# Layer 1's first gate and up tile: from the normalised stream to the residual scaled by channel, with root and shift put in behind

## The chip, the cores and the metric

The kernel runs on one core of one Trainium2 chip. The metric is the device time of one execution in microseconds (us). A core has a matrix engine (TensorE, PE in the profile; its weight loads are PEld), a vector engine (VectorE, DVE), an engine for scalar functions (ScalarE, ACT), a general one (GpSimd, POOL), a queue that issues the transfers (SyncE, SP), and 16 DMA engines. Each engine takes its instructions in the order in which the program put them, and waits where an operand is not there.

## The reference, cut to what matters

A two-layer diffusion transformer on 256 latent and 256 context tokens of 2048 channels. Layer 0 mixes by pooling, layer 1 by neighbourhood attention in which the latent tokens also read the context. Each layer then has a gated feed-forward part with a convolution of three tokens on the gate:

```python
def modulate(x, shift, scale):
    return x * (1 + scale) + shift

def conv_ffn(u, w_gate, w_up, conv_w, conv_b, w_down):
    T = u.shape[1]
    gp = jnp.pad(u @ w_gate, ((0, 0), (1, 1), (0, 0)))
    gte = gp[:, :T] * conv_w[0] + gp[:, 1:T + 1] * conv_w[1] + gp[:, 2:] * conv_w[2] + conv_b
    return (jax.nn.silu(gte) * (u @ w_up)) @ w_down

h = h + ml[:, 2] * y_lat                       # y_lat: the attention's output projection
h = h + ml[:, 5] * conv_ffn(modulate(rms_norm(h, norm2_g[i]), ml[:, 3], ml[:, 4]),
                            ffn_w_gate[i], ffn_w_up[i], ffn_conv_w[i], ffn_conv_b[i], ffn_w_down[i])
```

`rms_norm` divides each token by the root of its mean square and multiplies each channel by a gain. With s the gain times (1 + scale), r the reciprocal root of a token and b the shift, the feed-forward part reads r * (h * s) + b. So its product with a weight W is r * ((h * s) @ W) + b @ W. After layer 1 only the latent tokens are wanted. The gate and up weights have 5504 columns, the down weight 5504 rows.

## The kernel before, in words

Channels lie on the 128 partitions: a stream is 16 tiles of 128 channels by 256 tokens. The residual of the latent tokens, `hl`, stays in SBUF for the whole kernel. Every large product is split in two parts of lower precision: a weight is cast to a high part on ScalarE and the rest is taken off on VectorE, in some places on GpSimd (`split`, L147 and L149). The moving operand is kept as a pair too, high and low part side by side, 512 columns wide. A product with a weight tile of 128 columns is then 16 matmuls of the weight's high part with all 512 columns (here called wide) and 16 of its low part with the 256 high columns (narrow), in two halves of eight channel tiles each: eight wide, eight narrow, eight wide, eight narrow.

Weights come in halves of 512 KB over SP's queue into six staging buffers used in turn (`stage`, `load`). Split halves lie in three pairs of buffers (`whp`), and in three more (`whx`) once the attention's memory is free. PSUM has eight banks: four for gate, up and projections ("gu"), three and one for the rest.

A planner sorts the instructions of each engine at build time. It goes by the order in which the program wrote them and by its own times for when operands are there. `issue_after(x)` sets an instruction behind x on x's engine; `high_priority` lets one go ahead. The list `hold` puts the splits that follow behind given instructions.

Layer 1 runs like this. The attention goes through 16 pairs of heads (`kq_tile`: keys and queries, 3 x 16 and 16 + 16 matmuls); after every fourth pair the values of the next four follow (`v_group`). Keys and queries are rotated with one multiplication on GpSimd each (L937). The scores of a pair are worked off between the next pair's products. Then the output projection: 16 tiles `wo`, each with its update of `hl` (`o_end`, L1112). The last of them, tile 15, multiplies k by k and ends the attention.

The feed-forward norm follows the updates. `Norm.add` squares a tile on ScalarE (L297) and sums it on VectorE (L303). `Norm.rstd` sums over partitions on TensorE (L310), reduces (L313), scales (L314), raises to the power -1/2 on GpSimd (L315), puts the result on a diagonal (L318) and spreads it over all partitions on TensorE (L320). `norm_b` makes the 16 operands `B`: scale by channel and root on VectorE (L754), shift on ScalarE (L755), then the low part, for even tiles on VectorE (L761), for odd ones with one more ScalarE instruction on GpSimd (L758, L759).

`gu1(f)` does the gate and the up product of column tile f (L788 wide, L791 narrow), `gate1(f)` the convolution and the gating, and after every four tiles `down1` multiplies back. In tile 0 both weights are fetched and split ahead of `norm_b`; the splits of their second halves are held behind the last update of `hl` (`hold[:] = [tail]`, L774), those of tile 1 behind the normalised tile 9 (L764).

Of the kernel before, what the change touches and what calls it, by code (L numbers as in the profile page):

```python
# [13 lines left out]
ALU = mybir.AluOpType  # L14
# [45 lines left out]
def kernel(ctx: ExitStack, tc: tile.TileContext, xT, cxT, wmod, wg, wu, wd, wp,  # L60
# [18 lines left out]
    def flat(a):  # L79
        return a.rearrange("p s t -> p (s t)")  # L80
# [205 lines left out]
    class Norm:  # L286


        def __init__(self, streams, pool, name):
            self.streams, self.pool, self.name = streams, pool, name  # L290
            self.n = T * len(streams)
            self.acc = None

        def add(self, h_of, k):
# [439 lines left out]
    tail = _attention(tc, ap0, bank, ld, A, M, hl, wq, wv, wo, rope, strips, ident, v_first)  # L734

    with ExitStack() as ph2:
# [8 lines left out]
        for k in range(KT):  # L745
            n4.add(h_lat, k)
        rstd = n4.rstd()
        B = {}

        def norm_b(ks):  # L750
            for k in ks:
                a = ap0.tile([P, 2, 2, T], F32R, tag=f"A{k}", name=f"B{k}")[:, 0]
                y = f1.tile([P, 512], F32, tag="t2", name=f"nrmB{k}")[:, 0:T]
                nc.vector.scalar_tensor_tensor(y, hl[:, k, :], M(1, 4, k, 0), rstd[:, 0:T], op0=ALU.mult, op1=ALU.mult)  # L754
                nc.scalar.activation(a[:, 0], y, AF.Identity, bias=M(1, 3, k, 0))  # L755
# [8 lines left out]
                if k == 9:  # L764
                    hold[:] = [ins.ins]

        def gu1(f):
            res = []
            pre = None
            if f == 0:  # L770
                pre = [load(lambda a, b: w[1, f][:, a:b], 2048, f"w{nm}1_{f}") for nm, w in (("g", wg), ("u", wu))]
                for q, ts in enumerate(pre):
                    first = split(ts[:1], f"w{q}1_{f}_0", 4)
                    hold[:] = [tail]  # L774
                    pre[q] = first + split(ts[1:], f"w{q}1_{f}_1", 4)
                    hold.clear()
                norm_b(range(KT))
            elif f == 2:
                hold.clear()
            for q, (nm, wsrc) in enumerate((("g", wg), ("u", wu))):  # L780
                parts = pre[q] if pre else ld(wsrc[1, f], f"w{nm}1_{f}", 2 if f % 4 > 1 else 0)
                ps = bank("gu", f"{nm}1_{f}")

                for j in range(2):
                    hi, lo = parts[j]
                    for k in range(8 * j, 8 * j + 8):
                        c = P * (k % 8)
                        nc.tensor.matmul(ps, hi[:, c : c + P], flat(B[k]), start=(k == 0), stop=False)  # L788
                    for k in range(8 * j, 8 * j + 8):
                        c = P * (k % 8)  # L790
                        nc.tensor.matmul(ps[:, T:], lo[:, c : c + P], B[k][:, 0], start=False, stop=(k == KT - 1))  # L791
                res.append(ps)
            return res

        def gate1(f, banks):
            res = []
            for nm, ps in zip("gu", banks):
                e = f1.tile([P, 512], F32, tag="t2", name=f"e{nm}_{f}")[:, 0:T]
                nc.scalar.copy(e, ps[:, T:])
                nc.vector.tensor_tensor(e, e, ps[:, :T], op=ALU.add)  # L800
                res.append(e)
# [101 lines left out]
def _attention(tc, ap0, bank, ld, A, M, hl, wq, wv, wo, rope, strips, ident, v_first):  # L903
# [9 lines left out]
    with ExitStack() as es:  # L913
# [166 lines left out]
        for g in range(4):  # L1080
            v = v_group(g)
            for j in range(4):
# [5 lines left out]
                prev = v, P * j  # L1088
        queue.append(attend(KT - 1, *prev))
# [3 lines left out]
        def x_tile(k):  # L1093
            a = ap0.tile([P, 2, 2, T], F32R, tag=f"A{k}", name=f"oA{k}")[:, 0]
# [159 lines left out]
```

## Time and profile before

| what | value |
|---|---|
| median of three runs | 3057.1 us (3054.04 to 3058.71) |
| profiled execution, its own time | 3053.4 us |
| its span, first to last instruction | 3051.6 us |
| mean granted clock of TensorE | 0.991 |
| TensorE busy | 2974.9 us, 97% |
| VectorE, ScalarE, GpSimd busy | 1932.7, 1372.5, 827.9 us |
| attention's values, keys, queries | about 1690 to 2228 us of the span |
| output projection | about 2228 to 2305 us |
| first gate product of layer 1 | from 2313.12 us |

How to read it: a row of the timeline is the start in us, the duration, the engine, the line, the operation, what it writes and reads with their shapes, and how many instructions were merged. In brackets stands how long the engine had been idle before and which instruction released it. Buffer numbers are left out of names. In the rows of waits: who waited for whom, us in total, times, the longest. The granted clock is the share of full speed that TensorE was given. A busy TensorE counts pipelined matmuls, so times from start to start tell more than durations.

### The profile page before, as it was taken

To read this page: it belongs to the slowest core of one execution; us is meant where nothing else is said; L and a number is where in the kernel's file an instruction comes from. 1 tells how busy PE (TensorE), PEld (TensorE's weight loads), DVE (VectorE), ACT (ScalarE), POOL (GpSimd) and SP (SyncE) were. 2 spreads that over 40 slices of the span, in tenths; PEclk is the share of its full clock that TensorE was granted. 3 is DMA by queue.
4 is the path that set the end of the run, shared out by engine and by line. 5 is a ranking of instruction groups with operands and counts; after the bars stand their busy time and mean duration, and the time that the engine had idled before them with its cause. 6 is when DMAs were issued, how large, how long until landed. Compare 5 with 4: busy or idle time off the path is not lost.

```text
span 3051.6 us, 40877 instructions
## 1 busy us (share of the span) xinstructions
PE 2974.9 (97%) x15082; PEld 2414.5 (79%) x15082; DVE 1932.7 (63%) x2748; ACT 1372.5 (45%) x2219; POOL 827.9 (27%) x823
## 2 busy tenths in 40 slices
PE   5999999999999999999999999999999999999998
PEld 2666668888888888888887887878888888888887
DVE  4455664386584856748576656474767666666666
ACT  4333454324333232333434444343546666666665
POOL 2111313303123030221312000000002566566665
PEclk9999999999999999999999999999999999999999
DMA  9888663374665847557482333333355556655563
GB/s 391 322 308 318 213 213 103 110 249 147 205 202 164 249 137 228 173 186 223 147 251 76 117 100 116 100 106 112 107 162 186 186 185 192 190 186 185 183 194 115
DMA packets 177927, 559.70 MB, mean 183 GB/s; under 512 B 17600, under 2 KB 22208, under 8 KB 177728
## 3 DMA queue, kind: packets, MB, share of 16 engines
q1 hardware_dynamic: 177728, 557.10, 55.9%
q8 instruction: 119, 1.95, 0.2%
q14 instruction: 80, 0.66, 0.1%
HBM read 554.93 MB, written 2.10 MB: 183 GB/s over the span
## 4 chain that ended last, share of the span: by engine, by line
PE 91%; DVE 3%; DMA 3%; POOL 1%; issue 1%; ACT 1%; SPq 0%; DVEq 0%; POOLq 0%; ACTq 0%
PE g L788 5%; PE u L788 5%; PE d L679 5%; PE d L680 5%; PE d L681 5%; PE d L835 4%; PE g L653 4%; PE g L655 4%; PE g L654 4%; PE u L655 4%; PE u L653 4%; PE u L654 4%; PE g L791 3%; PE u L791 3%; PE d L839 2%; PE mod L206 2%
## 5 line engine op out<-in xcount | busy, mean ns | idle before, releaser
L692 POOL TENSOR_TENSOR hl<-hl,dy 128x256 f32<-128x256 f32 x160 | 146.7, 917 | 940.3 <-ACT dy L691 940.1
L850 POOL TENSOR_TENSOR hl<-hl,dy 128x256 f32<-128x256 f32 x320 | 331.6, 1071 | 188.4 <-ACT dy L848 186.1
L262 DVE SCALAR_TENSOR_TENSOR macc<-wm,sc,macc 128x512 f32<-128x512 f32 (+1 forms) x360 | 329.1, 946 | 68.6 <-DMA wm<-wmod 67.6
L691 ACT ACTIVATE dy<-d,modT 128x256 f32<-128x256 f32 x320 | 133.4, 470 | 187.5 <-PE d L681 168.0
L692 POOL TENSOR_TENSOR hc<-hc,dy 128x256 f32<-128x256 f32 x160 | 129.9, 812 | 0.0
L848 ACT ACTIVATE dy<-d,modT 128x512 f32<-128x512 f32 x160 | 104.6, 685 | 42.9 <-PE d L839 41.3
L149 DVE TENSOR_TENSOR wd_2l<-wd,wd_2h 128x1024 fp32r<-128x1024 f32 (+1 forms) x44 | 54.5, 1245 | 107.9 <-ACT wd_2h L147 106.7
L937 POOL TENSOR_TENSOR rk<-rk,rp 128x256 f32<-128x256 f32 x16 | 13.2, 827 | 365.9 <-DVE rk L936 310.2
L206 PE MATMUL mod<-wm,sc 128*32 128x512 f32 x768 | 97.7, 630 | 8.6 <-DMA wm<-wmod 8.4
L149 DVE TENSOR_TENSOR wd_3l<-wd,wd_3h 128x1024 fp32r<-128x1024 f32 (+1 forms) x44 | 52.0, 1202 | 77.7 <-ACT wd_3h L147 76.3
L149 DVE TENSOR_TENSOR wd_1l<-wd,wd_1h 128x1024 fp32r<-128x1024 f32 (+1 forms) x44 | 53.7, 1224 | 60.4 <-ACT wd_1h L147 60.4
L487 POOL TENSOR_TENSOR pf<-ws,inv 128x256 f32<-128x256 f32 x32 | 29.3, 937 | 211.1 <-DVE ws L482 200.8
L147 ACT CAST wd_1h<-wd 128x1024 fp32r<-128x1024 f32 (+1 forms) x44 | 45.3, 1032 | 81.2 <-PE u L654 55.1
L149 DVE TENSOR_TENSOR wd_0l<-wd,wd_0h 128x1024 fp32r<-128x1024 f32 (+1 forms) x44 | 54.6, 1247 | 36.4 <-ACT wd_0h L147 36.2
L1026 ACT ACTIVATE sb<-sb,nm 128x512 f32<-128x512 f32 x64 | 46.1, 721 | 64.3 <-DVE nm L1022 63.2
L147 ACT CAST wd_0h<-wd 128x1024 fp32r<-128x1024 f32 (+1 forms) x44 | 45.2, 1031 | 54.3 <-PE u L788 29.0
L814 DVE TENSOR_TENSOR actb<-sgb,actb 128x256 fp32r<-128x256 f32 x43 | 52.4, 1219 | 27.0 <-ACT actb L813 27.0
L679 PE MATMUL d<-act,wd_2h 128*128 128x512 f32 x172 | 67.1, 390 | 0.0
L680 PE MATMUL d<-act,wd_2h 128*128 128x512 f32 x172 | 66.9, 389 | 0.0
L681 PE MATMUL d<-act,wd_2l 128*128 128x512 f32 x172 | 66.9, 389 | 0.0
L679 PE MATMUL d<-act,wd_0h 128*128 128x512 f32 x172 | 66.9, 389 | 0.0
L680 PE MATMUL d<-act,wd_0h 128*128 128x512 f32 x172 | 66.9, 389 | 0.0
(1752 smaller groups left out, 9220.0 us busy)
## 6 DMA issues: line engine op xcount, KB each, us to landing
wm<-wmod SPq DMA_DIRECT2D x384, 512.0 KB, 6.1
wd<-wd SPq DMA_DIRECT2D x168, 512.0 KB, 4.5
wg<-wg SPq DMA_DIRECT2D x156, 512.0 KB, 4.6
wu<-wu SPq DMA_DIRECT2D x156, 512.0 KB, 4.6
wv<-wv SPq DMA_DIRECT2D x32, 512.0 KB, 3.8
wk<-wq SPq DMA_DIRECT2D x32, 512.0 KB, 3.9
wq<-wq SPq DMA_DIRECT2D x32, 512.0 KB, 3.7
wo<-wo SPq DMA_DIRECT2D x32, 512.0 KB, 4.0
```

The source lines that it names most:

```text
L149: eng.tensor_tensor(lo[:, :n], t[:, :n], hi[:, :n].bitcast(F32), op=ALU.subtract)
L262: nc.vector.scalar_tensor_tensor(acc[s], v, sc2[:, k, s : s + 1], acc[s], op0=ALU.mult, op1=ALU.add)
L653: nc.tensor.matmul(ps, hi[:, c : c + P], xh, start=(k == 0), stop=False)
L654: nc.tensor.matmul(ps, hi[:, c : c + P], xl, start=False, stop=False)
L655: nc.tensor.matmul(ps, lo[:, c : c + P], xh, start=False, stop=(k == KT - 1))
L679: nc.tensor.matmul(ps, hi[:, o : o + P], xh, start=(i == 0), stop=False)
L680: nc.tensor.matmul(ps, hi[:, o : o + P], xl, start=False, stop=False)
L681: nc.tensor.matmul(ps, lo[:, o : o + P], xh, start=False, stop=(i == n - 1))
L692: nc.gpsimd.tensor_tensor(h_of(s)[:, k, :], h_of(s)[:, k, :], y[:, s], op=ALU.add)
L788: nc.tensor.matmul(ps, hi[:, c : c + P], flat(B[k]), start=(k == 0), stop=False)
L791: nc.tensor.matmul(ps[:, T:], lo[:, c : c + P], B[k][:, 0], start=False, stop=(k == KT - 1))
L850: nc.gpsimd.tensor_tensor(hl[:, k, :], hl[:, k, :], y[:, q], op=ALU.add)
```

## The change

While the attention's output projection runs, each updated tile of `hl` is also multiplied by its channel scale and split into a high and a low part. These parts lie in the second half of the buffer whose first half holds the projection's own operand (`xs`). The first gate and up products read them. In the order on TensorE the sums of squares are put behind the first eight wide matmuls and the spread of the root behind the tenth. `norm_b` comes after that and writes its operands for the tiles from 1 on into the first halves. The last two squares are not summed on VectorE but go to TensorE as terms of their own, and the spread takes the root itself, broadcast, times the identity, so that the diagonal's step is gone.

Tile 0's gate and up results are then multiplied by the root and get the product of shift and weight as a bias. This product is made in the attention, once for the gate behind pair 6, once for the up weight behind pair 10 (`shift_row`): the weight tile is loaded once more, multiplied by the shift on GpSimd, added up there to 128 columns, summed over partitions on TensorE, and copied.

Besides: tile 0's splits are no longer held and all on VectorE, tile 1's gate weight is fetched ahead, tile 1 takes the first halves of gate and up before the second halves, and its up weight's split is placed behind tiles of `norm_b`.

```diff
+        def add_stream(self, h_of, k, s):
+            sq = self.pool.tile([P, 512], F32, tag="t2", name=f"{self.name}q{k}_{s}")[:, 0:T]
+            nc.scalar.activation(sq, h_of(s)[:, k, :], AF.Square)
+            if k >= KT - 2:
+                self.ends.setdefault(s, []).append(sq)
+            elif self.acc is None:
+                self.acc = sq
+            else:
+                v = self.acc[:, T * s : T * s + T]
+                nc.vector.tensor_tensor(v, v, sq, op=ALU.add)
+
+        def sums_of(self, s):
+            ps = bank("d", f"{self.name}s{s}")
+            terms = [self.acc[:, T * s : T * s + T]] + self.ends[s]
+            for j in range(2):
+                for i, sq in enumerate(terms):
+                    self.done = nc.tensor.matmul(ps[:, j : j + 1], sq[:, P * j : P * j + P], ones[:, 0:1],
+                                                 start=(i == 0), stop=(i == len(terms) - 1)).ins
+            v = main.tile([P, 4], F32, tag="normv", bufs=2, name=f"{self.name}v{s}")[:, :2]
+            nc.vector.tensor_scalar(v, ps[:, 0:2], 1.0 / D, EPS, op0=ALU.mult, op1=ALU.add)
+            nc.gpsimd.tensor_tensor(v, v, minus_half[:, :2], op=ALU.pow)
+            return v
+
+        def spread(self, s, v):
+            pb = bank("d", f"{self.name}b{s}")
+            for j in range(2):
+                self.done = nc.tensor.matmul(pb[:, P * j : P * j + P], v[:, j : j + 1].broadcast_to([P, P]), ident,
+                                             start=True, stop=True).ins
+            return pb
...
+    def shift_row(q):
+        ts = [t for t, _ in load(lambda a, b: (wg, wu)[q][1, 0][:, a:b], 2048, f"ws{q}")]
+        for j in range(4):
+            v = ts[j // 2][:, 512 * (j % 2) : 512 * (j % 2) + 512].rearrange("p (k c) -> p k c", k=4)
+            nc.gpsimd.tensor_tensor(v, v, modT[1, 12 + j][:, :, 0:1].broadcast_to([P, 4, P]), op=ALU.mult)
+        for j in range(2):
+            v = ts[0][:, 512 * j : 512 * j + 512]
+            nc.gpsimd.tensor_tensor(v, v, ts[1][:, 512 * j : 512 * j + 512], op=ALU.add)
+        for n in (512, 256, 128):
+            nc.gpsimd.tensor_tensor(ts[0][:, 0:n], ts[0][:, 0:n], ts[0][:, n : 2 * n], op=ALU.add)
...
+        ps = bank("d", f"wsum{q}")
+        nc.tensor.matmul(ps[:, 0:1], ts[0][:, 0:P], ones[:, 0:1], start=True, stop=True)
+        nc.vector.tensor_copy(sums[0][:, q : q + 1], ps[:, 0:1])
...
+        def first1():
+            raw = [load(lambda a, b: w[1, 0][:, a:b], 2048, f"w{nm}1_0") for nm, w in (("g", wg), ("u", wu))]
+            pre = [split(ts, f"w{q}1_0") for q, ts in enumerate(raw)]
+            ahead.append(ld(wg[1, 1], "wg1_1"))
...
+            for q in range(2):
+                ps = bank("gu", f"{'gu'[q]}1_0")
                 for j in range(2):
-                    hi, lo = parts[j]
+                    hi, lo = pre[q][j]
                     for k in range(8 * j, 8 * j + 8):
                         c = P * (k % 8)
-                        nc.tensor.matmul(ps, hi[:, c : c + P], flat(B[k]), start=(k == 0), stop=False)
+                        ins = product(ps, hi[:, c : c + P], flat(xs[k][:, 1]), start=(k == 0), stop=False)
+                        if (q, k) == (0, 7):
+                            with tc.issue_after(ins):
+                                v = n4.sums_of(0)
+                            last = n4.done
+                        if (q, k) == (0, 9):
+                            with tc.issue_after(ins):
+                                rstd.append(n4.spread(0, v))
+                            last = n4.done
+                            norm_b(range(KT))
                     for k in range(8 * j, 8 * j + 8):
                         c = P * (k % 8)
-                        nc.tensor.matmul(ps[:, T:], lo[:, c : c + P], B[k][:, 0], start=False, stop=(k == KT - 1))
+                        ins = product(ps[:, T:], lo[:, c : c + P], xs[k][:, 1, 0], start=False, stop=(k == KT - 1))
...
+            for q, j in ((0, 0), (1, 0), (0, 1), (1, 1)) if f == 1 else ((0, 0), (0, 1), (1, 0), (1, 1)):
+                part(q, j)
...
+                if f == 0:
+                    q = len(res)
+                    nc.vector.tensor_tensor(e, e, rstd[0][:, 0:T], op=ALU.mult)
+                    nc.scalar.activation(e, e, AF.Identity, bias=sums[0][:, q : q + 1])
...
+                if j == 2 and 1 <= g < 3:
+                    aside(g - 1)
...
+            a = xs[m][:, 1]
+            nc.scalar.activation(a[:, 0], hl[:, m, :], AF.Copy, scale=M(1, 4, m, 0))
+            nc.vector.scalar_tensor_tensor(a[:, 1], hl[:, m, :], M(1, 4, m, 0), a[:, 0].bitcast(F32),
+                                           op0=ALU.mult, op1=ALU.subtract)
```

`product` is a matmul put behind `last`, so all later matmuls of these two products stand behind the sums, and then behind the spread. `aside` is `shift_row`.

More of the change, by code (lines that the diff above doesn't have):

```diff
@@ L292, in __init__ @@
             self.acc = None
+            self.ends = {}
         def add(self, h_of, k):
@@ L763, in norm_b @@
                 B[k] = a
-                if k == 9:
-                    hold[:] = [ins.ins]
-        def gu1(f):
-            res = []
[L769 to L782, printed above, removed]
+                done_b.append((act.ins, ins.ins))
@@ L900, in _values, with _attention @@
                 nc.tensor.matmul(pv[i], xl, hi[:, c : c + 512], start=False, stop=(k == KT - 1))
[L903 removed]
+def _attention(tc, ap0, bank, ld, A, M, hl, wq, wv, wo, rope, strips, ident, v_first, xs, aside):
     nc = tc.nc
```

53 lines of the change are left out of this document (46 added, 7 removed).

## The prediction

> **What bounds the kernel now.** I read the page's busy table first, then TensorE's waits from the attention to the first tiles of layer 1's feed-forward part, then that seam in order of time.
>
> ```profile
> span 3051.6 us, 40877 instructions
> PE 2974.9 (97%) x15082; PEld 2414.5 (79%) x15082; DVE 1932.7 (63%) x2748; ACT 1372.5 (45%) x2219; POOL 827.9 (27%) x823
> ...
> PE g L788 <- DVE B L761: 2.2, 1, 2.2
> PE n4b L320 <- DVE n4d L318: 1.8, 1, 1.8
> PE n4s L310 <- ACT n4q L297: 1.5, 1, 1.5
> ```
>
> TensorE (PE) is the bound: 97% busy, 76.7 us of the span idle, and some of that idle time is here. The three waits belong to one chain, the norm ahead of layer 1's first gate product: squares (L297), sums (L310), root, spread (L320), then the first normalised tile (L761). The seam on TensorE:
>
> ```profile
> 2305.15 0.28 PE L1105 MATMUL op<-oA,wo15l 128*128 128x256 f32 x1
> 2305.26 0.53 PE L310 MATMUL n4s<-ones,n4q 128*128 128x1 f32 x4
> 2307.31 0.61 PE L310 MATMUL n4s<-ones,n4q 128*128 128x1 f32 x4 [1.51 <-ACT n4q L297]
> 2309.66 1.22 PE L320 MATMUL n4b<-n4d,ones 128*128 128x256 f32 x2 [1.75 <-DVE n4d L318]
> 2313.12 0.77 PE L788 MATMUL g<-B,w_0h 128*128 128x512 f32 x1 [2.23 <-DVE B L761]
> ...
> 2331.33 2.00 PE L788 MATMUL u<-B,wu_1h 128*128 128x512 f32 x8
> 2333.17 1.12 PE L791 MATMUL u<-B,wu_1l 128*128 128x256 f32 x8
> 2334.13 2.00 PE L788 MATMUL u<-B,wu_1h 128*128 128x512 f32 x8
> 2335.97 1.11 PE L791 MATMUL u<-B,wu_1l 128*128 128x256 f32 x8
> 2336.92 2.00 PE L788 MATMUL g<-B,wg_2h 128*128 128x512 f32 x8
> ...
> 2305.40:2313.20 7.80, 2.30 (x12) 1.44 (x10) 4.70 (x12) 3.34 (x8) 1.07 (x2) 0.75 0.50 174
> 2313.10:2316.30 3.20, 3.18 (x8) 2.54 (x9) 3.20 (x9) 3.20 (x10) 1.93 (x3) 0.52 0.00 0
> ```
>
> The attention's output projection ends at 2305.15 + 0.28 = 2305.43; the third pair of weight tiles (wg_2) begins at 2336.92. (In the two rows of stretches the columns are length, busy TensorE, weight load, VectorE, ScalarE, GpSimd, granted clock, DMA share, GB/s.) Between lie four products (gate and up of tiles 0 and 1) in 31.49 us. The whole product u of tile 1 takes 2336.92 - 2331.33 = 5.59, so four take 22.36. The excess is **9.13 us**: 2313.12 - 2305.43 = 7.69 before the first product, and 1.44 in which the clock came back (granted 0.52 from 2313.10 to 2316.30). From 2331.33 on, eight wide and eight narrow matmuls take 1.84 and 0.96.
>
> **The change, part by part.**
>
> *The seam.* The first two products read the residual times its channel scale, so they need neither root nor norm; the sums go in behind the eighth wide matmul, the spread behind the tenth. Can TensorE run on? Rows of the chain:
>
> ```profile
> 2306.84 0.41 ACT L297 ACTIVATE n4q<-hl 128x256 f32<-128x256 f32 x1
> 2307.95 0.16 DVE L313 TENSOR_REDUCE n4v<-n4s 128x2 f32<-128x4 f32 x1 [0.87 <-PE n4s L310]
> 2308.15 0.17 DVE L314 TENSOR_SCALAR n4v<-n4v 128x2 f32<-128x2 f32 x1
> 2308.40 0.70 POOL L315 TENSOR_TENSOR n4v<-n4v,minus_half 128x2 f32<-128x2 f32 x1 [7.51 <-DVE n4v L314]
> 2309.13 0.48 DVE L318 TENSOR_SCALAR n4d<-ident,n4v 128x128 f32<-128x128 f32 x2 [0.81 <-POOL n4v L315]
> 2310.93 1.65 DVE L754 SCALAR_TENSOR_TENSOR nrmB<-hl,modT,n4b 128x256 f32<-128x256 f32 x4 [1.31 <-PE n4b L320]
> 2312.89 0.86 DVE L754 SCALAR_TENSOR_TENSOR nrmB<-hl,modT,n4b 128x256 f32<-128x256 f32 x2
> 2314.07 0.86 DVE L754 SCALAR_TENSOR_TENSOR nrmB<-hl,modT,n4b 128x256 f32<-128x256 f32 x2
> ...
> 2225.76 0.67 PE pT L1035 x4
> ```
>
> Eight wide matmuls from 2305.43 end at 2307.27; the last square was there at 2307.25 even before, so the sums need not wait. They are 6 products (3 terms, 2 halves). Each shows as two instructions here (four products, eight instructions, 0.53 + 0.61), about 0.13 each: 12 x 0.13 = 1.6. The spread is two products of 128 columns, four instructions; the nearest rows are four 128-column instructions at 0.67 and, on the slow clock, 1.22 for L320. I take 0.6, since the clock stays up. **TensorE's added work is 2.2 us.** After the sums (2308.9) come eight narrow and two wide matmuls, 0.96 + 0.46, to 2310.3. The root needs L314, L315 and their hand-overs, 2309.10 - 2307.92 less L313's 0.2, so 1.0: ready at 2309.9, in time by 0.4. Behind one weight split on VectorE (DVE; 1.22 us, row below) it would be 0.8 late. I take 0, bounds 0 and 1.2.
>
> *The normalised tiles.* The spread ends at 2310.9, so L754 starts near 2311.0, as before. Sixteen tiles go in pairs of 2314.07 - 2312.89 = 1.18: 9.4 us, done at 2320.4, some 2 us later with the casts of tile 1's up weights put between on ScalarE (ACT). Tile 1 starts at 2305.43 + 11.18 + 2.2 = 2318.8, and now takes the first halves of both weights before the second: tiles 8 to 15 are wanted only from 2324.4. The cover is 2 us; without it, at worst 1.18 per pair that is late.
>
> *The weights of tile 0.* The old hold of the second halves behind the attention's last residual update goes; a half can still start only when a buffer of wo15's comes free.
>
> ```profile
> 2299.38 2.58 DVE L149 TENSOR_TENSOR wo15l<-wo,wo15h 128x1024 fp32r<-128x1024 f32 x1 [1.19 <-ACT wo15h L147]
> 2305.86 1.22 DVE L149 TENSOR_TENSOR w_1l<-wg,w_1h 128x1024 fp32r<-128x1024 f32 x1
> ...
> 2298.48 2.41 POOL L149 TENSOR_TENSOR w_1l<-wu,w_1h 128x1024 fp32r<-128x1024 f32 x1 [89.41 <-ACT w_1h L147]
> ...
> 1860.00:1935.00 75.00, 75.00 (x395) 59.22 (x395) 57.29 (x126) 35.83 (x69) 6.03 (x7) 1.00 0.36 111
> 1935.00:1995.00 60.00, 60.00 (x280) 49.28 (x278) 22.37 (x32) 19.76 (x28) 0.74 (x1) 1.00 0.30 98
> 2228.00:2300.00 72.00, 70.64 (x412) 61.81 (x409) 47.65 (x68) 34.53 (x45) 1.52 (x1) 1.00 0.58 183
> ```
>
> The gate's second half was split by 2305.86 + 1.22 = 2307.08 and is wanted only after the ninth wide matmul, past 2309.8. GpSimd (POOL) splits none of these now; VectorE gets that one (1.22) but loses the stretched 2.58. Nothing.
>
> *The scaled copies.* Each of 16 residual tiles gets one more ScalarE instruction (0.41, as L297) and one more VectorE instruction (0.48, as L318): 6.6 and 7.7 us in a stretch of 72 where they are busy 34.53 and 47.65. Covered; bare, the last tile's pair would cost 0.9. Tile 0's gate gets a multiplication and a bias per bank, four instructions behind TensorE; the banks are next wanted by tile 2, ten microseconds on. Nothing.
>
> *The shift's sums, inside the attention.* For gate and for up: two loads of 512 KB past the weights on SP, a chain on POOL, two 1-column instructions on TensorE (0.26), a small copy. The loads put 4 transfers between those of the next keys and queries, in the same six staging buffers. The chain is seven operations of 512 columns, one of 256, one of 128. The nearest rows:
>
> ```profile
> L937 POOL TENSOR_TENSOR rk<-rk,rp x16: 733/828/922, 1729.4 to 2194.5; 128x256 f32<-128x256 f32 x16
> ...
> 1901.67 0.91 POOL L937 TENSOR_TENSOR rk<-rk,rp 128x256 f32<-128x256 f32 x1 [14.76 <-DVE sm L1027]
> 1924.31 0.92 POOL L937 TENSOR_TENSOR rk<-rk,rp 128x256 f32<-128x256 f32 x1 [14.20 <-DVE rk L936]
> 1990.80 0.74 POOL L937 TENSOR_TENSOR rk<-rk,rp 128x256 f32<-128x256 f32 x1 [56.84 <-DVE rk L936]
> ...
> 1870.34 0.33 SPq L131 DMA_DIRECT2D wk<-wq  x1
> 1900.94 1.05 ACT L147 CAST wk7h<-wk 128x1024 fp32r<-128x1024 f32 x1 [0.67 <-ACT sb L1026]
> ```
>
> From 0.74 for 256 columns and 2.41 for 1024 I estimate 1.3 for 512 and 0.45 for 128: 7 x 1.3 + 0.74 + 0.45 = **10.3 us on POOL, twice**. The transfers cost nothing: DMA is at 0.36, and the second half of a key weight is asked for at 1870.34 and cast at 1900.94, so holding two of six buffers for 10 us uses up a third of a lead of 30. POOL is busy 6.03 of 75 us there and once sits idle for 56.84. The rotations queued behind it (rk, rq) feed scores that TensorE reaches microseconds later. The danger is TensorE's own queue: the 1-column product waits for POOL, and every key and query matmul stands behind it. Its wait is between 0 and 10.3 each time; I take 0, the nearest rows, since TensorE has not one wait between 1860 and 1995 (75.00 of 75, 60.00 of 60). With 2 x 0.26 = 0.5 the part costs 0.5.
>
> *The lock.* While POOL held 2298.48 to 2300.89, VectorE's split stretched from 1.22 to 2.58. [...] In the sum it stands at 0, and it is a rival below.
>
> **Sum:** 9.13 regained, 2.2 and 0.5 added: 6.4 us. The profiled execution's own time is 3053.4 (span 3051.6 and 1.8 around it), giving 3047.0; it lies 3.7 below the median of the three runs, 3057.1, from which I forecast **3050.7**.
>
> **The rivals.**
>
> *Part is given back (within 0.2%).* The root is 0.8 to 1.2 late behind a split, a pair of tiles 1.18 late, or the one-column product waits one or two microseconds. For it: the margins above are 0.4 and 2 us. Against it: each has a margin. Some 3 us back: 3053.7.
>
> *POOL's lock delays VectorE in the attention (within 0.2%).* Keys and queries of one head pair take 1924.31 - 1901.67 = 22.6 us, with VectorE idle (75 - 57.29) x 0.3 = 5.3. If POOL blocks it for all of 10.3 there, TensorE loses up to 5.0, twice: 3050.7 + 10 = 3060.7. Against it: after four pairs come 60 us with VectorE idle for 37.6, and POOL's operations fit between. [...]
>
> *TensorE waits for the shift's sums (slower).* If the one-column product stands in its queue before POOL is done, everything stops. It decides from 6.4 + 6.1 = 12.5 us on, 6.3 of the 10.3 each time. At 8 each: 3050.7 + 16 = 3066.7. For it: in the trace no TensorE instruction follows so long a POOL chain, so nothing shows that its place is late enough. Against it: POOL's long idle times.
>
> *The gap stays (within 0.2%).* The squares or scaled copies are late and TensorE waits all the same: 2.7 us at most is what the added work costs, 3059.8. Against it: the last square's 2307.25.
>
> **How the numbers follow.** Full closing 0.44; part given back 0.27; the lock 0.09; the queue 0.15; the gap stays 0.05. 0.2% is 6.1 us, about what a measurement of this kernel can tell from no change, and 6.4 is just above it: faster 0.44 and 0.01 of the second case, 0.45; within, the rest of the second, the lock and the gap that stays, 0.40; slower 0.15. The likeliest case alone runs from 3047 to 3053 (the three runs shown spread over 4.7). The range takes in all but the queue, with a run's spread below: 3046 to 3062.
>
> **What would show it.** The first gate matmul starts within 0.5 us of the projection's end and the granted clock stays near 1.00; wg_2 begins 24.6 us after that end instead of 31.5; no TensorE wait on the sums, the spread or B. In the attention, TensorE stays full in the stretches around the shift's sums, POOL showing some 10 us more in each of two. It is wrong if a TensorE wait on POOL's chain or on a delayed VectorE appears there, if the squares or root come late, or if something after tile 1 gives the time back.

## The result and the profile after

The changed kernel takes 3048.97 us (median of 11 runs, 3045.76 to 3052.48); beside it the kernel before took 3055.65 (11 runs, 3054.04 to 3059.88). The ratio is **0.9979 with a 95% interval of 0.9971 to 0.9986**, a gain of 6.7 us. The forecast was 6.4 us, 3050.7. When the changed kernel was measured once more (further down), one of its 11 executions took 3724.63 us at a mean granted clock of 0.751; the ratio given there leaves it out.

The profiled execution took 3052.48 us, with a span of 3050.7, just 0.9 below that of before, although the change is worth more. The busy table of the page, and the wait of TensorE that is left in the seam:

```profile
span 3050.7 us, 40962 instructions
PE 2976.8 (98%) x15092; PEld 2416.8 (79%) x15092; DVE 1949.0 (64%) x2765; ACT 1377.7 (45%) x2237; POOL 849.4 (28%) x840
```

```profile
PE n4s L324 <- ACT n4q L309: 0.9, 1, 0.9
```

Of the three waits of the old norm chain two are gone, those on the spread and on the first normalised tile. One wait on the sums (n4s) is left. The seam on TensorE's timeline:

```profile
2310.26 0.28 PE L1208 MATMUL op<-oA,wo15l 128*128 128x256 f32 x1
2310.39 2.00 PE L838 MATMUL g<-oA,w_0h 128*128 128x512 f32 x8
2312.23 0.50 PE L324 MATMUL n4s<-ones,n4q 128*128 128x1 f32 x4
2313.61 1.05 PE L324 MATMUL n4s<-ones,n4q 128*128 128x1 f32 x8 [0.88 <-ACT n4q L309]
2314.52 1.20 PE L838 MATMUL g<-oA,w_0l 128*128 128x256 f32 x8
...
2316.03 0.61 PE L335 MATMUL n4b<-ident,n4v 128*128 128x128 f32 x4
...
2335.58 2.00 PE L882 MATMUL g<-oA,wg_2h 128*128 128x512 f32 x8
```

The projection ends at 2310.26 + 0.28 = 2310.54, and the first gate matmul starts at 2310.39, before the last row of the projection is over. The third pair of weight tiles begins at 2335.58, so the seam takes **25.04 us where it took 31.49**: four products of 5.59 (22.36), 0.88 of waiting, and 1.80 for the sums and the spread. The granted clock is 1.00 in every stretch from 2310.00 to 2336.00 (a row of it stands under the run without shift sums).

Why did the span move by only 0.9? Add up the pieces: layer 0 ended later, by 1668.84 - 1663.98 = 4.86, in this execution, in code that the change does not touch (the power of the attention's norm on GpSimd marks it):

```profile
1663.98 1.02 POOL L315 TENSOR_TENSOR n3v<-n3v,minus_half 128x4 f32<-128x4 f32 x1 [35.75 <-DVE n3v L314]
```

```profile
1668.84 1.02 POOL L349 TENSOR_TENSOR n3v<-n3v,minus_half 128x4 f32<-128x4 f32 x1 [37.11 <-DVE n3v L348]
```

Behind it come -0.19 up to the fifth head pair, +0.44 from there to the projection's end (449.72 to 450.16), -6.45 in the seam and +0.44 in all the rest (714.68 to 715.12): together -0.90. So single spans mislead here, and every run below is read by its **seam** (projection's end to wg_2) and its **attention** (first rotation of the fifth head pair to the projection's end). Over all twelve further profiles that mark of layer 0 lay between 1662.1 and 1667.1, while the rest behind the seam stayed between 714.0 and 715.0.

The remaining wait is a matter of queue order. VectorE and ScalarE in the seam:

```profile
2309.95 1.22 DVE L149 TENSOR_TENSOR wg_1l<-wg,wg_1h 128x1024 fp32r<-128x1024 f32 x1 [1.27 <-ACT wg_1h L147]
2311.10 1.22 DVE L149 TENSOR_TENSOR w_0l<-wg,w_0h 128x1024 fp32r<-128x1024 f32 x1
2312.23 0.48 DVE L1219 SCALAR_TENSOR_TENSOR oA<-hl,modT,oA 128x256 fp32r<-128x256 f32 x1
2312.63 0.48 DVE L1215 SCALAR_TENSOR_TENSOR hl<-op,modT,hl 128x256 f32<-128x256 f32 x1
```

```profile
2308.87 1.05 ACT L147 CAST wg_1h<-wg 128x1024 fp32r<-128x1024 f32 x1 [2.63 <-DMA wg<-wg]
2309.83 1.04 ACT L147 CAST w_0h<-wg 128x1024 fp32r<-128x1024 f32 x1
...
2313.14 0.42 ACT L309 ACTIVATE n4q<-hl 128x256 f32<-128x256 f32 x1 [0.61 <-DVE hl L1215]
```

The last residual update (L1215) could start at 2310.54 but starts at 2312.63, behind two weight splits and the scaled copy of tile 14 (L1219). The splits were late because ScalarE stood 2.63 us for the transfer of tile 1's gate weights, with tile 0's second half queued behind that cast. The last square (2313.14) and the sums follow. The kernel before had the same two casts of tile 1's gate ahead of its last square (at 2303.01, after 2.40 us of standing, and at 2305.89). But VectorE took neither split ahead of the last update there; tile 0's second half followed it at 2305.86, tile 1's gate much later:

```profile
2305.47 0.48 DVE L1112 SCALAR_TENSOR_TENSOR hl<-op,modT,hl 128x256 f32<-128x256 f32 x1 [0.33 <-PE op L1105]
...
2317.62 2.35 DVE L149 TENSOR_TENSOR wg_1l<-wg,wg_1h 128x1024 fp32r<-128x1024 f32 x2
```

The shift's sums in the attention, first chain on GpSimd, then their product on TensorE (duration least, median, most; first and last start), then a stretch of TensorE around them:

```profile
1869.04 2.27 POOL L776 TENSOR_TENSOR ws<-ws,modT 128x512 f32<-128x512 f32 x2 [7.91 <-DMA strip<-strips]
...
1880.66 3.13 POOL L776 TENSOR_TENSOR ws<-ws,modT 128x512 f32<-128x512 f32 x2 [8.65 <-issue]
1883.76 2.73 POOL L779 TENSOR_TENSOR ws<-ws,ws 128x512 f32<-128x512 f32 x2
...
1888.12 2.74 POOL L781 TENSOR_TENSOR ws<-ws 128x512 f32<-128x512 f32 x3
```

```profile
L785 PE MATMUL wsum<-ones,ws x4: 250/260/272, 1911.5 to 2047.0; 128*128 128x1 f32 x4
```

```profile
1860.00:1935.00 75.00, 75.00 (x401) 59.00 (x399) 60.59 (x121) 36.95 (x69) 17.46 (x16) 1.00 0.43 130
```

GpSimd works 2.27 + 3.13 + 2.73 + 2.74 = 10.9 us and ends at 1890.86. TensorE takes the product at 1911.5, 20.6 us later, and is full in this stretch (75.00 of 75). The second chain takes 11.6 us and ends at 2025.44, some 21 us ahead of its product.

### The profile page after: what moved, and what is told of

Read it like the earlier page. It is cut to its first block, busy times and chain, and to the rows that moved or that the text cites. A ratio compares the mean times of both kernels' runs of the same rounds, so it can differ in the third digit from the quotient of the medians.

```text
span 3050.7 us, 40962 instructions
## 1 busy us (share of the span) xinstructions
PE 2976.8 (98%) x15092; PEld 2416.8 (79%) x15092; DVE 1949.0 (64%) x2765; ACT 1377.7 (45%) x2237; POOL 849.4 (28%) x840
## 4 chain that ended last, share of the span: by engine, by line
PE 91%; DMA 3%; DVE 3%; POOL 1%; issue 1%; ACT 1%; SPq 0%; DVEq 0%; POOLq 0%; ACTq 0%
PE g L882 5%; PE u L882 5%; PE d L713 5%; PE d L714 5%; PE d L715 5%; PE d L935 4%; PE g L687 4%; PE g L689 4%; PE g L688 4%; PE u L688 4%; PE u L689 4%; PE u L687 4%; PE g L885 3%; PE u L885 3%; PE d L939 2%; PE mod L206 2%
## 5 line engine op out<-in xcount | busy, mean ns | idle before, releaser
L206 PEld LDWEIGHTS mod<-wm,sc 128*32 128x32 f32 x768 | 21.7, 113 | 57.8 <-issue 55.1
L715 PE MATMUL d<-act,wd_0l 128*128 128x512 f32 x172 | 66.9, 389 | 0.0
```

The costliest lines, as they stand in the source:

```text
L715: nc.tensor.matmul(ps, lo[:, o : o + P], xh, start=False, stop=(i == n - 1))
```

## The experiments

Theory: the gain is the closed gap (7.69 us and the clock's 1.44), less what TensorE works more. The rivals asked whether something else in the change made it faster, and where the shift's sums could have cost.

**All of the change, but tile 0 waits for the normalised tiles.**

```diff
             last = None
+            rstd.append(n4.spread(0, n4.sums_of(0)))
+            norm_b(range(KT))
...
-                        ins = product(ps, hi[:, c : c + P], flat(xs[k][:, 1]), start=(k == 0), stop=False)
...
+                        ins = product(ps, hi[:, c : c + P], flat(B[k]), start=(k == 0), stop=False)
...
-                    nc.vector.tensor_tensor(e, e, rstd[0][:, 0:T], op=ALU.mult)
-                    nc.scalar.activation(e, e, AF.Identity, bias=sums[0][:, q : q + 1])
```

> The changed kernel, but the first gate and up products read the normalised tiles again and stand behind root and spread; scaled copies, shift's sums in the attention and the new order of the splits all stay. Theory (the gain is the closed gap): the seam, from the end of the output projection to the first matmul of wg_2, goes back from 25.0 to 31 or 32 us, and the time to within 1 us of the kernel before. Rival (the gain comes from the splits that are no longer held and from the new order of tile 1): the seam stays under 28 us.

Measured: 3057.64 us (10 runs), ratio 1.0007 (0.9997 to 1.0016). TensorE's waits, and a stretch behind the gap (columns as in the prediction's rows of stretches; the third number from the end is the granted clock):

```profile
PE n4s L324 <- ACT n4q L309: 2.9, 2, 2.0
PE g L840 <- DVE oA L818: 2.2, 1, 2.2
...
PE n4b L335 <- POOL n4v L328: 1.0, 1, 1.0
```

```profile
2317.80:2321.00 3.20, 3.19 (x8) 2.52 (x9) 3.20 (x9) 3.20 (x10) 1.91 (x3) 0.50 0.00 0
```

The three waits are back and the clock falls to 0.50 behind them. The seam is 33.81, 8.77 above the changed kernel's; the ratios differ by 0.0028, 8.6 us. So the gain lies in tile 0's independence from the norm; the other parts of the change bring nothing by themselves. The seam is even 2.3 us longer than in the kernel before, past the theory's 31 or 32: the gap is 9.76 us where it was 7.69, with the sums waiting 2.9 us for the squares instead of 1.5, and the time lies 1.7 us above the kernel before instead of within 1.

**The kernel before with TensorE kept busy in the gap** by six matmuls into an unused bank, one behind the first sums, two behind the sums, three behind the spread.

```diff
+    def fill(behind, n):
+        if not filled:
+            filled.append(bank("gu", "fill"))
+        with tc.issue_after(behind), tc.high_priority():
+            for i in range(n):
+                nc.tensor.matmul(filled[0], ones, flat(hl[:, 0:2, :]), start=(i == 0), stop=(i == n - 1))
...
```

> The kernel before with six matmuls that nothing reads put into TensorE's gaps of the seam (one after the first sums, two before the spread, three after it). Theory (1.44 us of the excess of 9.13 are a clock that fell because TensorE idled): the granted clock stays near 1.00, the first 7 wide matmuls take 0.23 instead of 0.43 us each, the seam goes from 31.5 to about 30.1 us. Rival (the clock falls whatever fills the gap, or the filling delays the chain by as much): the seam stays at 31.5 us or grows.

Measured (one run beside one of before): 3052.8 against 3055.15; the seam is 29.58 us. The stretch behind the gap:

```profile
2314.00:2317.20 3.20, 3.20 (x15) 2.64 (x15) 3.20 (x9) 3.20 (x10) 1.95 (x3) 1.00 0.00 0
```

The granted clock stays at 1.00 where before had 0.52. Of the 1.91 us regained, 0.58 is a shorter gap (7.69 to 7.11) and 1.33 the clock: behind the gap 29.58 - 22.36 - 7.11 = 0.11 is left of 1.44. The term for the clock holds, by one run of each kernel.

**The kernel before with its splits neither held nor on GpSimd.**

```diff
-                    first = split(ts[:1], f"w{q}1_{f}_0", 4)
-                    hold[:] = [tail]
-                    pre[q] = first + split(ts[1:], f"w{q}1_{f}_1", 4)
+                    first = split(ts[:1], f"w{q}1_{f}_0")
+                    pre[q] = first + split(ts[1:], f"w{q}1_{f}_1")
```

> The kernel before with only the splits changed: those of tile 0's second halves no longer held behind the last residual update, and none of tile 0's on GpSimd. Theory (the norm's chain sets the seam): the seam stays within 0.7 us of 31.5. Rival (the held splits set it): it falls by 2 us or more.

Measured (one run): 3054.22 against 3055.15; the seam is 31.08, 0.41 under before, a sixteenth of the gain. Where the splits go was not the cause. The last update starts 0.31 us behind the projection's end here (0.04 in the kernel before), so taking the hold away does not by itself make it late.

**Without the shift's sums:** tile 0 leaves out the product of shift and weight.

```diff
-                    nc.scalar.activation(e, e, AF.Identity, bias=sums[0][:, q : q + 1])
...
-                if j == 2 and 1 <= g < 3:
-                    aside(g - 1)
```

> The changed kernel without the shift's sums: no extra load, no chain on GpSimd, no bias in tile 0 (the product of shift and weight is left out of the result there). Theory (the chain lies beside other work): from the rotation that opens the second group of four pairs (rk of pair 4) to the end of the projection 449.6 us instead of 450.2, the time 0 to 1 us below the changed kernel's. [...]

Measured: 3047.91 us (10 runs), ratio 0.9976 (0.9967 to 0.9985), not to be told from the changed kernel. The attention takes 449.73, as before, so the two chains together cost 450.16 - 449.73 = 0.43. The seam was a surprise: 26.48, 1.4 longer than with the sums, though the wait on n4s was 0.81. Its timeline and stretch, and the same stretch of the changed kernel (second fence):

```profile
2308.70 1.05 PE L324 MATMUL n4s<-ones,n4q 128*128 128x1 f32 x8 [0.81 <-ACT n4q L309]
2309.62 2.05 PE L838 MATMUL g<-oA,w_0l 128*128 128x256 f32 x8
...
2309.00:2312.00 3.00, 3.00 (x17) 2.90 (x17) 0.89 (x3) 0.05 (x1) 0.70 (x1) 0.60 0.83 247
```

```profile
2313.60:2316.60 3.00, 2.99 (x23) 2.91 (x24) 1.19 (x3) 0.35 (x1) 0.71 (x1) 1.00 0.89 255
```

Eight narrow matmuls took 2.05 instead of 1.20: the granted clock fell to 0.60 behind the short wait. This comes up again with the longer chain below and in the last section.

**The shift's sums in the seam**, ahead of the first gate product.

```diff
-                if j == 2 and 1 <= g < 3:
-                    aside(g - 1)
...
+            for q in range(2):
+                shift_row(q)
             res = []
```

> The changed kernel with the shift's sums moved from the attention to the seam, behind the splits of tile 0. Theory (the chain is free in the attention only because VectorE has spare time there; at the seam VectorE is full and the lock costs): VectorE's splits there stretch from 1.22 to over 2 us, root, normalised tiles or weights come late, and the seam grows by 3 to 15 us over 25.0. Rival (the lock costs little wherever the chain stands): the seam stays under 27 us.

Measured: 3067.95 us (4 runs), ratio 1.0041 (1.0028 to 1.0055).

```profile
PE wsum L785 <- POOL ws L781: 16.7, 2, 14.7
```

The seam is 45.49, 20.4 us longer, past the 3 to 15 that were expected. VectorE's splits stretch as the theory said (to 2.07 and 1.89 us, from 1.22), but most of the time is TensorE standing at the one-column product. So the prediction's rival in which it does so came about here, at 16.7 us of waiting; in the changed kernel the place in the attention, with more than 20 us of lead, is what avoids it.

**A longer chain:** 24 multiplications by one, of 512 columns, are added to each of the two.

```diff
+        for _ in range(6):
+            for j in range(4):
+                v = ts[j // 2][:, 512 * (j % 2) : 512 * (j % 2) + 512].rearrange("p (k c) -> p k c", k=4)
+                nc.gpsimd.tensor_tensor(v, v, ones[:, 0:1].unsqueeze(1).broadcast_to([P, 4, P]), op=ALU.mult)
         for j in range(2):
             v = ts[0][:, 512 * j : 512 * j + 512]
```

> The changed kernel with 24 more multiplications by one, 512 columns each, in each of the two chains on GpSimd: 25 to 31 us more of GpSimd's time, twice, in the attention. TensorE's 1-column product came 20.6 us after the end of the first chain. Theory (VectorE's spare time and that margin cover it): from rk of pair 4 to the end of the projection 450 to 456 us, TensorE waiting on GpSimd or the 1-column product by at most 5 us in all. Rival (the lock passes every blocked microsecond of VectorE on to TensorE): 465 us or more.

Measured (one run): 3058.09 against 3055.15; the attention takes 462.00, 11.8 more, between the theory's 450 to 456 and the rival's 465. TensorE's waits in it, and the first stretch:

```profile
PE pT L1139 <- DVE sb L1132: 5.4, 3, 2.7
PE s L1116 <- DVE pt L1140: 1.6, 1, 1.6
```

```profile
1860.00:1935.00 75.00, 72.27 (x372) 56.69 (x371) 67.36 (x121) 34.47 (x66) 47.64 (x40) 0.98 0.37 119
```

TensorE does not wait for the one-column product but for VectorE, whose same 121 instructions now take 67.36 us instead of 60.59. This fits the lock rival, though not at its full price. GpSimd's own queue is a second way for the delay, which this run does not separate: the rotation of the next keys, behind the longer chain, starts 6.85 us after its operand is ready (1875.93 to 1882.78), where that took 4.18 in the changed kernel (1882.26 to 1886.44). GpSimd's work in the stretch grew by 47.64 - 17.46 = 30.2 us, and 5.9 us per chain, a fifth of it, came through. At the real length all of it costs 0.43 for two chains.

The seam is 26.94 here, and the clock fell in it as in the run without the shift's sums. TensorE waited 1.26 us at the sums, and the eight narrow matmuls behind them took 1.61 instead of 1.20, the two wide ones after that 1.06 instead of 0.63; from 2319.70 to 2322.70 the granted clock was 0.59.

```profile
2319.71 1.61 PE L842 MATMUL g<-oA,w_0l 128*128 128x256 f32 x8
```

**The sums and the spread later:** behind the tenth and the sixteenth wide matmul.

```diff
-                        if (q, k) == (0, 7):
+                        if (q, k) == (0, 9):
                             with tc.issue_after(ins):
                                 v = n4.sums_of(0)
...
-                        if (q, k) == (0, 9):
+                        if (q, k) == (0, 15):
```

> The changed kernel with the sums behind the tenth wide matmul instead of the eighth and the spread behind the sixteenth instead of the tenth. Theory: the wait of 0.88 us on the last square goes, since the sums come 1.4 us later; but the normalised tiles start later as well, and their cover, about 2 us by the prediction, decides: if it holds, the seam is 24.2 us. Rival: the cover is smaller, TensorE waits on B or on tile 1's weights by as much as it saved or more, and the seam is 25.0 us or longer.

Measured (one run): 3048.21 against 3055.15; seam 25.29, none gained.

```profile
PE g L882 <- POOL oA L816: 1.1, 1, 1.1
```

The wait on the sums is gone, and the last normalised tile, made on GpSimd (L816), is late by 1.1 instead. The cover of the normalised tiles is nearly used up as it stands.

**Tile 1's gate split behind the last residual update.**

```diff
+            hold[:] = [tail]
             ahead.append(ld(wg[1, 1], "wg1_1"))
+            hold.clear()
```

> The changed kernel with one thing more: VectorE's split of tile 1's gate weight is put behind the last update of the residual. Theory (the 0.88 us that TensorE waits for the sums come from a split ahead of that update on VectorE): the wait on the last square goes to 0, the seam from 25.0 to 24.2 us, 0.9 us less in all. Rival (the square is late because TensorE's projection ends late and the hand-overs take that long): the wait stays above 0.5 us. Rival 2: the split is then late itself and TensorE waits on it or on B.

Measured: 3046.94 us (11 runs), ratio 0.9977 (0.9968 to 0.9986). The seam is 26.43 and the wait on the sums 1.54, longer; a second wait, of 0.49, stands at the spread. ScalarE and VectorE show why:

```profile
2306.00 1.05 ACT L147 CAST wg_1h<-wg 128x1024 fp32r<-128x1024 f32 x1 [3.48 <-DMA wg<-wg]
2306.96 1.04 ACT L147 CAST w_0h<-wg 128x1024 fp32r<-128x1024 f32 x1
```

```profile
2308.03 1.23 DVE L149 TENSOR_TENSOR w_0l<-wg,w_0h 128x1024 fp32r<-128x1024 f32 x1 [2.95 <-ACT w_0h L147]
...
2309.57 0.48 DVE L1217 SCALAR_TENSOR_TENSOR hl<-op,modT,hl 128x256 f32<-128x256 f32 x1
```

The moved split was only half the matter. ScalarE still stands with tile 1's cast at the head of its queue, so tile 0's second half is late, and VectorE holds that split ahead of the update. The theory named only one of the two splits; the wait stayed above 0.5 us as in the first rival, but not for its reason.

**Both queues reordered:** tile 1's casts behind the last square; on VectorE, tile 0's second halves and tile 1's gate behind the last update.

```diff
+            for q, ts in enumerate(raw):
+                first = split(ts[:1], f"w{q}1_0_0")
+                hold[:] = [tail]
+                pre.append(first + split(ts[1:], f"w{q}1_0_1"))
+                hold.clear()
...
+            hold[:] = [n4.squared, tail]
+            ahead.append(split(next_g[:1], "wg1_1_0"))
...
+                            hold[:] = [n4.squared, n4.scaled]
+                            ahead[0] += split(next_g[1:], "wg1_1_1")
```

> The kernel after with another order on two queues: the cast of tile 1's gate weights, which stands at the head of ScalarE's queue while their transfer is awaited, is put behind the last square of the residual, and VectorE's subtractions for the second half of tile 0's weights and for tile 1's gate behind the last residual update. Theory (in the kernel after, ScalarE stood 2.63 us before tile 1's cast, VectorE's splits stood behind it and the last residual update behind them, and that is the 0.88 us that TensorE waited at the sums): the last update begins within 0.8 us of the projection's end instead of 2.1, the wait on the sums is 0 to 0.2 us, the seam is 24.2 us (bounds 24.0 to 24.6) where it was 25.04. Rival: tile 1's gate weights or the normalised tiles now come late in their place, TensorE waits there, and the seam is 25.0 us or more.

Measured: 3048.83 us (11 runs), ratio 0.9978 (0.9969 to 0.9987); seam 25.78.

```profile
PE n4b L335 <- POOL n4v L328: 1.5, 1, 1.5
```

```profile
2308.80 0.48 DVE L1226 SCALAR_TENSOR_TENSOR hl<-op,modT,hl 128x256 f32<-128x256 f32 x1 [0.94 <-PE op L1219]
...
2311.86 1.22 DVE L149 TENSOR_TENSOR wg_0l<-wg,wg_0h 128x1024 fp32r<-128x1024 f32 x1
2313.00 0.15 DVE L327 TENSOR_SCALAR n4v<-n4s 128x2 f32<-128x2 f32 x1
```

The update now starts 0.05 us behind the projection's end (2308.75) and the wait on the sums is gone. Its cause is shown: the order of the two queues, taken together. But a split stands ahead of the root's first step (L327), and TensorE waits 1.5 at the spread: the rival's outcome by a third wait in the same queue.

**The changed kernel again,** beside that run.

> The kernel after once more, beside the one above. Theory: the wait on the sums is there in every execution, 0.7 to 1.0 us long, and the seam is 25.0 us (24.8 to 25.3) at a granted clock of 1.00. Rival (the clock falls in some executions after that wait, as in the run without the shift's sums): the seam is 26.4 us, with a granted clock of 0.6 to 0.85 in the 6 us behind the projection's end.

Measured: 3047.18 us (11 runs), ratio 0.9976 (0.9967 to 0.9985). The seam is 25.23, the wait on the sums 1.1, and the granted clock 1.00; the theory's seam came, the wait slightly above its bound. Neither profile of this kernel shows the fall of the clock.

**Tile 1's splits behind the root's first step as well** (the diff is against the run with both queues reordered).

```diff
-            hold[:] = [n4.squared, tail]
-            ahead.append(split(next_g[:1], "wg1_1_0"))
-            hold.clear()
...
-                            ahead[0] += split(next_g[1:], "wg1_1_1")
+                            ahead.append(split(next_g, "wg1_1"))
```

> The run e10_queue_order with one step more: both of VectorE's subtractions for tile 1's gate stand behind the addition of the epsilon to the mean of the squares (they stood behind the last residual update alone, and there one of them, 1.14 us long from 2311.86, ran ahead of that addition at 2313.00, for which TensorE then waited 1.5 us). Theory (the order of VectorE's queue alone made both waits): the addition runs within 0.2 us of the last sum, neither the sums nor the spread of the root keep TensorE waiting over 0.3 us, and the seam is 24.2 us (bounds 24.0 to 24.7). Rival (the chain of addition, root and spread is itself longer than the ten products set behind the sums): a wait of 0.4 us or more stands at the spread though no split is ahead of the root, and the seam is 24.7 us or more.

Measured: 3047.38 us (7 runs), ratio 0.9973 (0.9962 to 0.9984); seam 24.68, at the upper bound of the theory. TensorE's only wait in the seam, over the theory's 0.3, then GpSimd's power and VectorE's splits:

```profile
PE n4b L335 <- POOL n4v L328: 0.4, 1, 0.4
```

```profile
2310.53 1.63 POOL L328 TENSOR_TENSOR n4v<-n4v,minus_half 128x2 f32<-128x2 f32 x1 [98.93 <-DVE n4v L327]
```

```profile
2310.37 2.36 DVE L149 TENSOR_TENSOR wg_1l<-wg,wg_1h 128x1024 fp32r<-128x1024 f32 x2
```

VectorE's queue was the cause of 1.1 of the 1.5. The 0.4 left is the rival's: a chain that is too long, because the power takes 1.63 beside a split where it takes 0.71 alone (in the changed kernel).

**The spread two wide matmuls later,** to fill that (the diff is against the run above).

```diff
-                        if (q, k) == (0, 9):
+                        if (q, k) == (0, 11):
```

> The run e11_split_behind_root with the spread of the root behind the twelfth wide matmul where it stood behind the tenth. There TensorE still waited 0.43 us at the spread, because the power on GpSimd took 1.63 us beside a split on VectorE, where it takes 0.71 alone. Theory: two more wide matmuls, 0.46 us, fill that wait, the spread comes at the same time as before, the normalised tiles are no later, no wait over 0.1 us is left between the projection's end and the third pair of weight tiles, and the seam is 24.2 us (bounds 24.1 to 24.4). Rival: the normalised tiles move back with the spread and the wait appears at tile 1's second halves, seam 24.6 us or more.

Measured: 3046.83 us (9 runs), ratio 0.9974 (0.9964 to 0.9984); seam 24.64.

```profile
2324.99 0.50 PE L890 MATMUL g<-oA,wg_1h 128*128 128x512 f32 x1 [0.17 <-POOL oA L816]
```

The wait at the spread is gone, another of 0.17 stands at tile 1's second half, and of 0.4 us 0.04 is gained. The rival was right: the normalised tiles are the next bound. These last two variants save 0.4 to 0.6 us of the seam, which their times can't tell from the changed kernel's.

## Why the prediction came out right, step by step

- *The gap closes.* Right. The first gate matmul stands right behind the projection, two of the three waits are gone and the clock stays at 1.00. Forecast for the seam: 24.6; it is 25.04 and 25.23. One of the forecast's signs of being wrong, squares that come late, did show, at 0.88 us. Taking tile 0's independence away alone gives all of it back.
- *The clock's 1.44.* Right: filling the gap without closing it brings 1.33 of it.
- *TensorE's added work, 2.2.* Mis-sized: 1.80. Without a wait the 12 instructions of the sums pass in 2311.52 - 2310.26 = 1.26 (run with later sums; 1.6 forecast), and the spread in 2316.39 - 2316.03 = 0.36 (0.6).
- *"So the sums need not wait".* This step failed, by 0.88 us. It took the last square's time from the old trace, where tile 0's second halves were held behind the last update. The change took that hold away and set VectorE's split of tile 1's gate ahead of that update as well; the forecast's "Nothing" for the weights of tile 0 did not ask what would now run ahead of it. That this is the cause is shown by the reordered queues, where the wait is gone. The work's size gives part of it back: 2.2 forecast against 1.80 + 0.88 = 2.68.
- *The root in time by 0.4, 0.8 late behind a split.* No wait in the changed kernel, where the sums come late enough for the splits to be over (the last ends at 2313.02 + 1.21 = 2314.23, the power starts at 2314.94). The margin of 0.4 did not count that the power takes longer beside a split: in the run with nothing ahead of the root on VectorE it was 0.43 late, since the power took 1.63 (0.71 in the changed kernel). Behind a split it was 1.5 late, not 0.8.
- *Cover of 2 us for the normalised tiles.* Wrong, and by luck without a cost here. In the changed kernel:

```profile
2316.67 1.65 DVE L811 SCALAR_TENSOR_TENSOR nrmB<-hl,modT,n4b 128x256 f32<-128x256 f32 x4 [1.82 <-PE n4b L335]
```

```profile
2327.67 0.74 POOL L816 TENSOR_TENSOR oA<-nrmBz,oA 128x256 fp32r<-128x256 f32 x1 [0.46 <-ACT nrmBz L815]
2328.87 1.56 POOL L816 TENSOR_TENSOR oA<-nrmBz,oA 128x256 fp32r<-128x256 f32 x1 [0.46 <-ACT nrmBz L815]
```

```profile
2329.05 1.99 PE L882 MATMUL g<-oA,wg_1h 128*128 128x512 f32 x8
```

The tiles start at 2316.67 and the last is ready at 2328.87 + 1.56 = 2330.43: 13.8 us, not 9.4 + 2. The forecast left out the last tile's way over ScalarE and GpSimd, and its last step took 1.56 instead of 0.74. TensorE reads that tile with the eighth of the wide matmuls that begin at 2329.05, at 0.23 each about 2330.7. Some 0.2 us of cover is left of the 2, which is why moving the sums or the spread back uncovers a wait.
- *The scaled copies, nothing.* Right but for one. Without the shift's sums, yet with the copies, attention and projection take 449.73, as before (449.72). The copy of tile 14 stands 0.40 us ahead of the last update.
- *The shift's sums, 0.5 on TensorE, 10.3 on GpSimd each.* Right: 0.43, and 10.9 and 11.6.
- *The rivals.* The queue rival needs the product within reach of the chain; it is 20.6 us away, and with the chain in the seam the kernel was 12 us slower than before. The lock costs 0.43 at most at this length; with some 30 us more per chain, lock and queue on GpSimd cost 11.8 together. That a chain holds VectorE up for all of its length, as the rival's 5.0 per chain has it, no run shows: beside the longer chain VectorE's 121 instructions took 67.36 us instead of 60.59. The gap did not stay, though its mechanism, a late square, is the one that gave 0.88 back. Part was given back, though by another step than named, and less: 0.88 of 3.
- *The sum.* 6.45 - 0.44 = 6.0 in the trace against 6.4 forecast; by the ratios 6.4 (0.9979) and 7.3 (0.9976, the second time). The intervals (0.9971 to 0.9986 and 0.9967 to 0.9985) leave no doubt of a gain; whether it lies above or below the 0.2% of the forecast's chances they leave open. Part of the agreement is luck. Less work on TensorE than forecast paid for half of the wait that was not forecast, the cover that the forecast put at 2 us was 0.2 and just enough, and the clock stayed up, while in two variants it fell behind a similar wait and cost some 1.5 us.

## What to carry to other kernels

When a chain of small steps (sums, root, spread) stands between two streams of matmuls and its result is only a factor per token and a sum per column, put the products first and the chain behind them; here that closed the gap (7.69 us) and saved the 1.44 us in which the clock came back behind it (granted 0.52), for 1.80 us of added work and a wait of 0.88. Then look at the in-order queues of the engines that feed the chain: a weight split that depends on a late transfer, placed ahead of the last update, delayed everything behind it here, and each wait taken away showed the next (sums, root, spread, normalised tiles). Side work for GpSimd was nearly free here (0.43 us for two chains), with a VectorE that had idle time (60.59 us busy of 75 around the first chain) and a consumer on TensorE more than 20 us behind it; a chain of some 40 us was not (11.8 us for two).

## What was not expected of the hardware

- The granted clock fell in two variants behind one short wait with one-column sums on both sides. Without the shift's sums it fell to 0.60 behind a wait of 0.81 us (2.2 us from 2307.40 to 2309.62 with the sums), and with the longer chain to 0.59 behind 1.26 us; each cost some 1.5 us (the seams of 26.48 and 26.94 less 22.36 for the products, 1.80 for sums and spread, and the wait). The changed kernel with a wait of 0.88 or 1.1, and another run with 1.54, kept 1.00, so the length of the wait alone does not decide. What does, no run here shows.
- The power of two columns on GpSimd takes 0.70 to 0.71 us alone (the changed kernel, twice, and several variants) and 1.62 to 1.64 while VectorE splits weights (the last three variants). In the run with tile 1's splits behind the root's first step, the first split began at 2310.37 and the power at 2310.53. Two splits take 2.36 there and one 1.22 elsewhere, so the first was over some 1.14 after its start and 0.98 after the power's; 0.98 + 0.71 = 1.69 lies near the 1.63 measured, as if the power had done its work behind that split. That is an estimate; no run shows what held the power.
- The time of one unchanged stretch, layer 0, varies by up to 6.8 us between executions (its end lies between 1662.1 and 1668.8), as much as the change is worth.
